# A hybrid attention/retention inference step: one more pair of channel tiles as seven products, parked sums of x through a buffer half as large

## The chip, the cores and the metric

The kernel runs on one core of a Trainium2 chip. The metric is device time in microseconds (us); the kernel before takes 1887.12 us, the median of three runs (1886.89 to 1887.62). The profiled execution took 1887.63 us, of which the profile's span, from the first instruction to the last, is 1885.9 us.

## What is computed

One encoder layer on 2048 new frames (the prompt) and 64 frames of a running stream (the sample): a norm, one wide input projection, differential attention, retention, gates, and the output projections. All data are float32. Cut to what matters here:

```python
D_MODEL, SEQ, DEC_SEQ = 1024, 2048, 64
h = rmsnorm(x, norm_g) @ w_in                       # 6144 columns in all
qa, ka, va, za, qb, kb, vb, zb, ga, gb = split(h)   # za, zb: silu gates; ga, gb: merge gates
oa = diff_attention(rmsnorm(qa), rmsnorm(ka), va)   # block-causal, 4 heads
ob = retention(qb, kb * DK_B ** -0.5, vb)           # chunkwise recurrent, 4 heads
oa = rmsnorm(oa) * (1 - lam_init) * silu(za)
ob = rmsnorm(ob) * silu(zb)
m  = sigmoid(ga + b_gate[0]) * (oa @ w_oa) + sigmoid(gb + b_gate[1]) * (ob @ w_ob)
y  = x + m @ w_out
```

The change concerns the projection columns qb, kb, za, zb, ga and gb: 16 blocks of 256 columns, called pairs here since each is two tiles of 128 channels. They are produced transposed, channels on the partitions and frames along the row.

## The kernel before

**Products.** A float32 value is held as a high and a low part (`h` and `l`, or `wh`, `wl`, `xh`, `xl`), made by a cast on ScalarE (ACT) and a subtraction on VectorE (DVE) or GpSimd (POOL). A float32 product is three matmuls: high by high, high by low, low by high.

**Stages.** The frames are worked in two halves of 1024; the second half also carries the 64 sample frames, so it has 1088 columns: 512 and twice 288. In each half the input projection runs (`w_stream`), and attention and retention (`z_stream`) fill in between its matmuls. After the second half the out stream follows (`out_stream`, L2935): gates, `m`, and `y`.

**Pairs in the first half** are all made by `strassen` (L958) with seven products of sums in place of eight blocks. The sums of weight blocks t1 to t4, formed on POOL in `sum_prep` (L805), are stored to a DRAM tensor `wsum` by `sum_keep` (L866) for those pairs that will need them again: the pairs from number `PLAIN` on.

**Pairs in the second half.** The first `PLAIN` = 11 pairs are made plainly by `transposed` (L1426, matmuls at L1137): for each of the two channel tiles, 8 blocks of the contraction and three matmuls each, over columns of 512, 288 and 288. The last five are made together by `quad` (L1544, matmuls at L1564): seven phases, in the order of `PHASES`, one product of sums each. In a phase each pair has one weight piece (`wh`, `wl`) of 4 blocks and two column groups, of 256 and of 288 columns: 12 matmuls into one bank for each. Between phases the sums stay in SBUF buffers `u256` and `u288`, 11 of each.

**What follows a product.** `q_p6` to `q_p3` (L1600 to L1650) read the bank: the first phase, S2, by a copy on ACT (L1591), the second, A11, by a copy and a DVE add (L1584), the others by one DVE add, the fifth, S3, by two. The adds go to `u` or to an evacuation tile `ev` that a DMA then stores.

**Sums of x.** `x_again` (L1479) forms the eight operands of x on POOL while attention runs and parks them in a DRAM tensor `xd`. `x_pass` (L1510) brings them back, phase by phase. The first phase's operand (S2) arrives already split. For each other phase one load (`xraw<-xd`, 1088 KB) lands in `xraw`, [128, 2176]; once one of the two slots of `xh`/`xl` is free (`xfree`, given when a phase's last matmul has been issued), four pieces of 544 are split: cast on ACT (L1526), subtraction on DVE (L1529). `quad` waits at the head of each phase for the finished slot.

**Other work around that place.** When attention has ended, `out_prep` and `load_wout` begin to prepare the out stream beside the products: `on<-on,z` (L2609 on POOL, L2615 on DVE), `ogl` (L2626), and the output weights' low parts (L2473 on POOL, L2477 on DVE). The low parts of the weight pieces (`next_sub`, L747) go to whichever of DVE and POOL the planner's own clock shows less loaded.

**What sets the order.** The instruction order of PE, ACT and DVE is written out by hand-made generators under a small planner: `loop` (L197) picks the task of lowest priority number that is ready by its clock, which advances by assumed costs (`P`, `A`, `V`, `G`, `ld`, `st`, L258 to L288). On the chip each engine takes its instructions strictly in that order. All loads and stores go out on one queue, SP's, in order.

Of the kernel before, what the change touches and what calls it, by code (L numbers as in the profile page):

```python
# [8 lines left out]
F32 = mybir.dt.float32  # L9
# [59 lines left out]
OPERANDS = [("b11", 0, 0), ("t2", 2, 1), ("t3", 0, 1), ("b21", 1, 0), ("t1", 2, 0), ("t4", 0, 0), ("b22", 1, 1)]  # L69


PLAIN = 11
SPREAD = 6000.0
PHASES = [("t2", "S2", "q_p6"), ("b11", "A11", "q_p1"), ("b21", "A12", "q_p2"), ("t1", "S1", "q_p5"),
          ("t3", "S3", "q_p7"), ("t4", "A22", "q_p4"), ("b22", "S4", "q_p3")]
NAMES = ("S2h", "A22", "A11", "A12", "S1", "S3", "S4", "S2l")
# [96 lines left out]
class Hybrid:  # L173
# [631 lines left out]
    def sum_prep(self):  # L805
# [17 lines left out]
        pair = len(self.sunits) - 1 + self.sdone  # L823
        keep = pair >= PLAIN
        left = [11 if keep else 7, 0.0]
# [600 lines left out]
    def transposed(self, dst, d0, scale, grouped):  # L1426
# [6 lines left out]
        self.nplain += 1  # L1433
        if self.nplain == PLAIN:
            order = [(ct, k) for k in (1, 2, 0) for ct in range(2)]
        for ct, k in order:
# [7 lines left out]
                                     (ct, k) == order[-1])  # L1444
            if self.nplain == PLAIN and (ct, k) == (1, 2):
                self.seg1_done = self.pe + LAT
# [63 lines left out]
    def x_pass(self):  # L1510
        self.xslots, self.xfree, self.parked, self.xraw = [], [(1, 0.0)], -1, None
        yield lambda: self.parked == 1 and self.seg1_done is not None
        yield max(self.seg1_done, self.kept)
        for k, (_, name, _) in enumerate(PHASES):
            if k == 0:
                for j, x in enumerate(self.x_slot(0)):
                    t = self.ld(x.bitcast(F32), self.xd[:, 7 * j].rearrange("p c t -> p (c t)"), 1114112)
                self.xslots.append((0, t))
                yield lambda: self.xraw is not None
                continue  # L1520
            t = self.ld(self.xraw, self.xd[:, NAMES.index(name)].rearrange("p c t -> p (c t)"), 1114112)
            s = yield from self.ring(self.xfree)
            yield t
            h, l = self.x_slot(s)
            for c in range(0, 2176, 544):
                self.nc.scalar.copy(h[:, c:c + 544], self.xraw[:, c:c + 544])  # L1526
                t = self.A(544, self.pe)
                yield t
                self.nc.vector.tensor_sub(l[:, c:c + 544], self.xraw[:, c:c + 544], h[:, c:c + 544].bitcast(F32))  # L1529
                t = self.V(644, t)  # L1530
            self.xslots.append((s, t))
            yield t

    def u_room(self):

        self.zx.close()
        pool = self.z2.enter_context(self.tc.tile_pool(name="sums", bufs=1))
        self.xraw = pool.tile([128, 2176], F32, tag="xraw", name="xraw")
        self.ufree = []
        for n in WIDTH:  # L1540
            u = pool.tile([128, 11 * n], F32, tag=f"u{n}", name=f"u{n}")
            self.ufree.append([(u[:, n * k:n * k + n], 0.0) for k in range(11)])

    def quad(self, pairs):  # L1544

# [1415 lines left out]
    def w_stream(self):  # L2961
# [31 lines left out]
        later = [(vb, lambda half: self.natural(half, self.fin_vb(), False, True), True)]  # L2993
        plain = [(c0, lambda half, a=a: self.transposed(*a), False) for c0, a in again[:PLAIN]]
        c0s, args = zip(*again[PLAIN:])
        seqs = [first + early + seq, [plain[0], wide[0], plain[1], wide[1], wide[2], m0, m1, plain[2], plain[3],
# [4 lines left out]
        for half in range(2):  # L3001
            for c0, wide in self.order[half]:
                if half:
                    self.pieces += [(wide,)] * {True: 8, False: 4, "quad": 7 * (16 - PLAIN)}[wide]
                else:
# [197 lines left out]
```

## Time and profile before

| | |
|---|---|
| runs | 1886.89, 1887.12, 1887.62 us |
| profiled execution, its own time | 1887.63 us |
| span of its profile | 1885.9 us |
| between the two | 1.73 us |
| granted TensorE clock over the span | 1.0 of full speed |
| DVE, ACT, POOL busy | 1330.5, 975.9, 669.5 us |
| matmuls of the plain pairs (L1137, `mm<-xh,wh`) at 288 columns | 352, mean 303 ns each |
| matmuls of the product block (L1564) | 840, from 1419.07 to 1532.1 us |

How to read it: a matmul's listed duration contains the pipeline behind it, so that 840 matmuls of some 290 ns overlap and cannot be added. What one costs the engine is the distance between starts. The engines' busy times are sums over stages with different limits, so a change in one stage is read from that stage: here the stretch from about 1380 us, where attention ends, to 1532 us, where the out stream starts.

### The profile page before, as it was taken

Reading aid. Unit: us, or ns where it says so; the run is one execution under the profiler, and the core shown is the slowest. Engines: PE = TensorE matmul, PEld = TensorE weight load, DVE = VectorE, ACT = ScalarE, POOL = GpSimd, SP = SyncE. Lnnn points to the kernel's source line nnn. Section 1 sums busy time; section 2 is a strip of 40 time slices with the busy share of each in tenths; the row PEclk is TensorE's granted clock in tenths of the full one; section 3 lists DMA queues with packets and bytes.
Section 4 is the critical chain, followed back from the end, with each engine's and each line's share of the span. In section 5 each row is a group of like instructions: output and inputs, shape, how many; then the busy total and the mean of one; then the engine's idle time right before and its main releaser. Section 6 shows DMA issues by size and latency. Waiting matters only on the chain.

```text
span 1885.9 us, 33029 instructions
## 1 busy us (share of the span) xinstructions
PE 1867.0 (99%) x11090; PEld 1644.9 (87%) x11090; DVE 1330.5 (71%) x3117; ACT 975.9 (52%) x2266; POOL 669.5 (36%) x723
## 2 busy tenths in 40 slices
PE   9999999999999999999999999999999999999999
PEld 7788878888888789888988889899999899998887
DVE  6765857658585677787587777677866969977664
ACT  6444545554434566556465655556666436654221
POOL 2420266555552122022210344243224625512442
PEclk9999999999999999999999999999999999999999
DMA  7664555666867967556423649446437988886452
GB/s 258 209 177 122 162 165 169 177 199 198 243 185 191 254 196 191 154 170 174 139 73 95 178 131 244 120 130 158 115 115 231 284 233 257 271 237 209 165 157 77
DMA packets 402555, 340.07 MB, mean 180 GB/s; under 512 B 85329, under 2 KB 348625, under 8 KB 401362
## 3 DMA queue, kind: packets, MB, share of 16 engines
q1 hardware_dynamic: 402386, 337.97, 61.7%
q8 instruction: 87, 1.43, 0.3%
q14 instruction: 82, 0.67, 0.1%
HBM read 218.27 MB, written 118.75 MB: 179 GB/s over the span
## 4 chain that ended last, share of the span: by engine, by line
PE 89%; DMA 4%; DVE 4%; issue 1%; SPq 1%; ACT 1%; POOL 0%; DVEq 0%; ACTq 0%; POOLq 0%
PE mm L1137 29%; PE mm L989 8%; PE tp L989 4%; PE at L1990 3%; PE s L1879 2%; PE s L1878 2%; PE s L989 2%; PE pv L1970 2%; PE pv L1969 2%; PE pv L1968 2%; PE mm L1564 1%; PE s L2793 1%; PE s L2795 1%; PE s L2794 1%; PE pv L2256 1%
## 5 line engine op out<-in xcount | busy, mean ns | idle before, releaser
L748 POOL TENSOR_TENSOR wl<-ws,wh 128x512 fp32r<-128x512 f32 x102 | 142.5, 1408 | 240.8 <-ACT wh L727 160.2
L1137 PE MATMUL mm<-wh,xh 128*128 128x512 f32 x504 | 203.0, 403 | 0.0
L1137 PE MATMUL mm<-wh,xl 128*128 128x512 f32 x504 | 198.1, 393 | 0.0
L1137 PE MATMUL mm<-wl,xh 128*128 128x512 f32 x504 | 198.0, 393 | 0.1
L1137 PE MATMUL mm<-xh,wh 128*128 128x288 f32 (+2 forms) x544 | 179.8, 330 | 0.0
L1137 PE MATMUL mm<-xh,wl 128*128 128x288 f32 (+2 forms) x544 | 175.5, 323 | 0.0
L1137 PE MATMUL mm<-xl,wh 128*128 128x288 f32 (+2 forms) x544 | 175.5, 323 | 0.0
L1918 ACT ACTIVATE row<-row,a_mx 128x1024 f32<-128x1024 f32 (+7 forms) x144 | 149.8, 1042 | 11.7 <-DVE a_mx L1897 11.7
L2006 DVE TENSOR_TENSOR atl<-at,ath 128x512 fp32r<-128x512 f32 (+1 forms) x144 | 92.6, 658 | 77.8 <-ACT ath L2004 77.6
L2004 ACT CAST ath<-at 128x512 fp32r<-128x512 f32 (+1 forms) x144 | 79.1, 564 | 106.2 <-PE at L1990 105.7
L856 POOL TENSOR_TENSOR wl<-ws,wh 128x256 fp32r<-128x256 f32 x64 | 55.3, 865 | 197.8 <-ACT wh L847 197.6
L1745 POOL TENSOR_TENSOR r_y<-r_y,r_sq 128x256 f32<-128x256 f32 x32 | 29.7, 929 | 236.2 <-DVE r_sq L1742 152.4
L1137 PEld LDWEIGHTS mm<-wh,xl 128*128 128x128 f32 x504 | 94.6, 188 | 21.6
L1137 PEld LDWEIGHTS mm<-wl,xh 128*128 128x128 f32 x504 | 95.0, 188 | 18.4 <-POOL wl L748 0.9
L1137 PEld LDWEIGHTS mm<-wh,xh 128*128 128x128 f32 x504 | 94.9, 188 | 17.8 <-DVE raw L1308 0.2
L1137 PEld LDWEIGHTS mm<-xh,wh 128*128 128x128 f32 x544 | 102.4, 188 | 7.2
L1137 PEld LDWEIGHTS mm<-xl,wh 128*128 128x128 f32 x544 | 102.5, 188 | 6.9
L1137 PEld LDWEIGHTS mm<-xh,wl 128*128 128x128 f32 x544 | 102.3, 188 | 6.6
L1887 DVE CUSTOM_DVE_ANT_0 row<-s,dfar 128x512 f32<-128x512 f32 (+2 forms) x141 | 87.0, 629 | 23.4 <-PE s L1879 16.8
L1940 DVE SCALAR_TENSOR_TENSOR row<-row,a_w 128x1024 f32<-128x1024 f32 (+5 forms) x88 | 97.3, 1111 | 0.0
L727 ACT CAST wh<-ws 128x512 fp32r<-128x512 f32 x111 | 67.7, 619 | 47.9 <-DMA ws<-wsum 13.2
L1878 PE MATMUL s<-K,q 128*128 128x512 f32 (+3 forms) x240 | 90.5, 379 | 1.3 <-DVE a_acc L1887 1.3
(543 smaller groups left out, 6072.4 us busy)
## 6 DMA issues: line engine op xcount, KB each, us to landing
ws<-in_w_in_dram SPq DMA_DIRECT2D x155, 256.0 KB, 3.4
q<-qT SPq DMA_DIRECT2D x128, 128.0 KB, 3.8
K<-kT SPq DMA_DIRECT2D x48, 256.0 KB, 4.6
V<-vN SPq DMA_DIRECT2D x24, 512.0 KB, 5.9
row<-in_x_prompt_dram SPq DMA_DIRECT2D x16, 512.0 KB, 4.5
wz<-in_w_in_dram SPq DMA_DIRECT2D x32, 256.0 KB, 4.3
row<-in_cache_k_T_dram SPq DMA_DIRECT2D x32, 256.0 KB, 3.2
row<-in_cache_v_diff_dram SPq DMA_DIRECT2D x32, 256.0 KB, 3.6
```

The lines of the kernel that those rows point to most:

```text
L727: self.nc.scalar.copy(h, st)
L748: eng.tensor_sub(l, st, h.bitcast(F32))
L856: nc.gpsimd.tensor_sub(l[:, cs], src, h[:, cs].bitcast(F32))
L989: nc.tensor.matmul(ps, w[:, c], xs[x][c], start=bool(tag) and c == 0 and i == 0, stop=c == 3 and i == 2, skip_group_check=True)
L1137: nc.tensor.matmul(ps, p, q, start=c == 0 and i == 0, stop=c == KC - 1 and i == 2)
L1878: nc.tensor.matmul(ps, q1s, kk, start=True, stop=False)
L1887: nc.vector.tensor_tensor_reduce(out=row[:, k0:k0 + n], in0=ps, in1=tab, scale=-SLOPES[h], scalar=3.0e38, op0=ALU.add, op1=ALU.min, accum_ ...
L1918: nc.scalar.activation(u, u, AF.Exp, bias=mx, scale=-1.0, accum_out=lp[:, k:k + 1])
L1940: nc.vector.scalar_tensor_tensor(out=u0, in0=u1, scalar=w[:, 0:1], in1=u0, op0=ALU.mult, op1=ALU.add)
L1990: nc.tensor.transpose(at[:, w:w + 128], src, self.ident)
L2004: nc.scalar.copy(ah[:, :w], at[:, :w])
L2006: nc.vector.tensor_sub(al[:, :w], at[:, :w], ah[:, :w].bitcast(F32))
```

## The change

`PLAIN` goes from 11 to 10: pair number 10, two tiles of `ga`, leaves the plain pairs and joins the product block, which then has six pairs. Its sums t1 to t4 are kept in `wsum` in the first half (four more stores of 256 KB), and in the second half its weights come as seven pieces of [128, 4, 128] rather than four of [128, 2, 256]. Each phase has six pairs, 144 matmuls, where it had 120. The `u` buffers go from 11 to 13 of each width; to make room `xraw` goes from 2176 to 1088 columns, and `x_pass` brings each operand in two loads, the second of which overwrites the first one's buffer, so it is issued after the first one's two pieces have been split.

```diff
-PLAIN = 11
+PLAIN = 10
@@ x_pass
-            t = self.ld(self.xraw, self.xd[:, NAMES.index(name)].rearrange("p c t -> p (c t)"), 1114112)
-            s = yield from self.ring(self.xfree)
-            yield t
-            h, l = self.x_slot(s)
-            for c in range(0, 2176, 544):
-                self.nc.scalar.copy(h[:, c:c + 544], self.xraw[:, c:c + 544])
-                t = self.A(544, self.pe)
+            for a in (0, 1088):
+                t = self.ld(self.xraw, self.xd[:, NAMES.index(name)].rearrange("p c t -> p (c t)")[:, a:a + 1088], 557056)
+                if a == 0:
+                    s = yield from self.ring(self.xfree)
+                    h, l = self.x_slot(s)
                 yield t
-                self.nc.vector.tensor_sub(l[:, c:c + 544], self.xraw[:, c:c + 544], h[:, c:c + 544].bitcast(F32))
-                t = self.V(644, t)
+                for c in (0, 544):
+                    x = self.xraw[:, c:c + 544]
+                    self.nc.scalar.copy(h[:, a + c:a + c + 544], x)
+                    t = self.A(544, self.pe)
+                    yield t
+                    self.nc.vector.tensor_sub(l[:, a + c:a + c + 544], x, h[:, a + c:a + c + 544].bitcast(F32))
+                    t = self.V(644, t)
+                yield t
             self.xslots.append((s, t))
-            yield t
@@ u_room
-        self.xraw = pool.tile([128, 2176], F32, tag="xraw", name="xraw")
+        self.xraw = pool.tile([128, 1088], F32, tag="xraw", name="xraw")
...
-            u = pool.tile([128, 11 * n], F32, tag=f"u{n}", name=f"u{n}")
-            self.ufree.append([(u[:, n * k:n * k + n], 0.0) for k in range(11)])
+            u = pool.tile([128, 13 * n], F32, tag=f"u{n}", name=f"u{n}")
+            self.ufree.append([(u[:, n * k:n * k + n], 0.0) for k in range(13)])
```

The lines after the change lie three further down in the file (L1564 becomes L1567, L1584 becomes L1587), and the split's L1526 and L1529 become L1529 and L1532.

On TensorE the order is the same up to the second of the last two plain pairs before the block, and the same again from the first matmul of the out stream on. Between, attention (queries by keys, `s<-K,q`) is found inside the product block, where before only its last transposes and value products reached into the block. Before, at the block's first matmul (`L1990` are the attention's transposes, `L1968` to `L1970` its products with V):

```order
L1968 MATMUL pv<-ath,V 128x256
L1969 MATMUL pv<-ath,V 128x256
L1970 MATMUL pv<-atl,V 128x256
L1990 MATMUL at<-ident,row 128x128 x3
L1564 MATMUL tp<-xh_122,wh 128x256
L1564 MATMUL tp<-xl_123,wh 128x256
L1564 MATMUL tp<-xh_122,wl 128x256
L1564 MATMUL tp<-xh_122,wh 128x256
```

After the change, in the block's first phase:

```order
L1567 MATMUL mm<-xl_123,wh 128x256
L1567 MATMUL mm<-xh_122,wl 128x256
L1881 MATMUL s<-K,q 128x512
L1882 MATMUL s<-K,q 128x512
L1881 MATMUL tp<-K,q 128x512
L1882 MATMUL tp<-K,q 128x512
L1567 MATMUL mm<-xh_122,wh 128x256
L1567 MATMUL mm<-xl_123,wh 128x256
```

72 matmuls of the block stand before the attention's last rows in the old order and 768 behind them; now it is 264 and 744.

On DVE the splits of x lie differently among the adds. Before, the four splits for phase A22, while phase S3 runs:

```order
L1529 TENSOR_TENSOR xl_123<-xraw,xh_122 128x544
L1584 TENSOR_TENSOR u_16726<-at,u_16726 128x256
L1529 TENSOR_TENSOR xl_123<-xraw,xh_122 128x544
L1584 TENSOR_TENSOR ev<-at,u_16726 128x256
L1584 TENSOR_TENSOR u_16727<-at,u_16727 128x288
L1529 TENSOR_TENSOR xl_123<-xraw,xh_122 128x544
L1584 TENSOR_TENSOR ev<-at,u_16727 128x288
L1584 TENSOR_TENSOR u_16726<-mm,u_16726 128x256
L748 TENSOR_TENSOR wl<-ws,wh 128x512
L1529 TENSOR_TENSOR xl_123<-xraw,xh_122 128x544
```

After the change, the last two of the four splits for that phase and what stands ahead of them:

```order
L1587 TENSOR_TENSOR ev<-mm,u_16215 128x288
L1587 TENSOR_TENSOR ev<-mm,u_16214 128x256
L1587 TENSOR_TENSOR u_16215<-s,u_16215 128x288
L748 TENSOR_TENSOR wl<-ws,wh 128x512
L1587 TENSOR_TENSOR ev<-s,u_16215 128x288
L1587 TENSOR_TENSOR u_16214<-s,u_16214 128x256
L1532 TENSOR_TENSOR xl_123<-xraw,xh_122 128x544
L2618 TENSOR_TENSOR on<-on,z 128x528
L1587 TENSOR_TENSOR u_16215<-at,u_16215 128x288
L1587 TENSOR_TENSOR ev<-s,u_16214 128x256
L1532 TENSOR_TENSOR xl_123<-xraw,xh_122 128x544
```

The splits come in two twos, and the last two stand behind more of the phase's adds. From the row after the last split for phase S1 to the last split for phase A22, the work beside phases S1 and S3, DVE has 46 rows before the change (24 adds from banks and 22 operations between SBUF tiles) and 65 after it (37 and 28); from there to the last split for S4 it has 24 rows before and 22 after (12 and 10). In the last phase-long piece ahead of A22 alone, after the change, there are 24 adds and 14 of the others.

On SP's queue, the loads of x for S3 (`gbT<-ev` are stores of finished tiles, `ws` weight pieces, `z`, `on` and `wst` for the out stream). Before, one row among the others:

```order
L280 DMA ws<-wsum 128x4x128
L280 DMA xraw<-xd 128x2176
L285 DMA gbT<-ev 128x4x8
L285 DMA gbT<-ev 128x256
L280 DMA ws<-wsum 128x4x128
L285 DMA gbT<-ev 128x256
```

After, the first load, the second one, and what lies between them:

```order
L280 DMA xraw<-xd 128x1088
L285 DMA gbT<-ev 128x256
L280 DMA ws<-wsum 128x4x128
L285 DMA gbT<-ev 128x4x8
L285 DMA gbT<-ev 128x256
L280 DMA z<-zbT 128x2x264
L280 DMA on<-obT 128x2x264
L280 DMA ws<-wsum 128x4x128
L280 DMA wst<-in_w_o_diff_dram 128x2x256
L280 DMA ws<-wsum 128x4x128 x2
L280 DMA xraw<-xd 128x1088
```

Ten transfers for other users stand between the two.

## The prediction

> **What bounds the kernel now.** I read the page first, then the chain of waits, then PE's waits and the stretches of the product block.
>
> ```profile
> span 1885.9 us, 33029 instructions
> PE 1867.0 (99%) x11090; PEld 1644.9 (87%) x11090; DVE 1330.5 (71%) x3117; ACT 975.9 (52%) x2266; POOL 669.5 (36%) x723
> PE 89%; DMA 4%; DVE 4%; issue 1%; SPq 1%; ACT 1%; POOL 0%; DVEq 0%; ACTq 0%; POOLq 0%
> ```
>
> The reader sees an engine that is hardly ever idle: 1885.9 - 1867.0 = 18.9 us over the whole span, and a chain that is PE for 89%. So fewer matmul columns shorten the run, unless PE then has to wait. Of that idle time the product block holds this (its waits, then its stretches: PE, PEld, DVE, ACT and POOL busy, clock, DMA share, GB/s):
>
> ```profile
> PE mm L1564 <- DVE ev L1584: 2.1, 1, 2.1
> PE s L1564 <- DVE xl L1529: 1.6, 1, 1.6
> PE s L1564 <- DVE u L1584: 0.9, 1, 0.9
> ...
> 1460.00:1480.00 20.00, 20.00 (x161) 19.97 (x160) 15.67 (x24) 10.35 (x18) 8.68 (x7) 1.00 0.84 238
> 1480.00:1500.00 20.00, 17.49 (x132) 16.57 (x130) 20.00 (x28) 11.07 (x19) 17.86 (x11) 1.00 1.10 330
> 1500.00:1520.00 20.00, 18.00 (x143) 18.03 (x144) 16.78 (x31) 8.15 (x15) 9.23 (x7) 1.00 1.05 274
> ```
>
> Three waits, 2.1 + 1.6 + 0.9 = 4.6 us, all on DVE, which in 1480 to 1500 us is busy without a gap. The third 2 us, in 1500 to 1520, are the wait on `ev`; elsewhere in the block PE is full. So the block has two limits close together: PE, and in phases S1 and S3 the DVE.
>
> **The change part by part. Matmuls.** What one costs is the distance between starts, twelve apart in a row:
>
> ```profile
> 1403.72 0.39 PE L1137 MATMUL mm<-xh,wl 128*128 128x512 f32 x1
> ...
> 1406.44 0.39 PE L1137 MATMUL mm<-xh,wl 128*128 128x512 f32 x1
> ...
> 1442.07 0.28 PE L1564 MATMUL mm<-xh,wh 128*128 128x256 f32 x1
> ...
> 1443.49 0.30 PE L1564 MATMUL mm<-xh,wh 128*128 128x288 f32 x1
> ...
> 1445.09 0.28 PE L1564 MATMUL s<-xh,wh 128*128 128x256 f32 x1
> ```
>
> That is 2.72/12 = 0.227 us at 512 columns, 1.42/12 = 0.118 at 256, 1.60/12 = 0.133 at 288. Removed: 2 tiles x 8 blocks x 3 = 48 at 512 and 96 at 288, 10.9 + 12.8 = 23.7 us. Added: 7 x 12 = 84 at 256 and 84 at 288, 9.9 + 11.2 = 21.1 us. Net **-2.6 us**: the seven-for-eight ratio gives 3 us, and shorter matmuls give 0.4 back. A phase becomes 6 x (1.42 + 1.60) = 18.1 us long; it was 15.1.
>
> **First half.** Four more stores of 256 KB, and one pair's raw weights held until they land. PE has no wait on a weight there today; the sums of the pairs after this one are kept in the same way. Nothing; if that cover failed, one load's time of some 4 us once.
>
> **Attention inside the block.** 192 more of the block's matmuls stand ahead of attention's end and take the place of the plain ones there in PE time (192 x 0.126 = 24 us against 23.7). Beside them ACT and DVE get copies and adds that the plain pairs hadn't. Between 1400 and 1440 us DVE was idle for half:
>
> ```profile
> 1400.00:1420.00 20.00, 20.00 (x129) 17.98 (x128) 9.38 (x19) 9.89 (x20) 6.77 (x5) 1.00 0.33 88
> 1420.00:1440.00 20.00, 20.00 (x163) 19.98 (x162) 8.94 (x13) 12.39 (x30) 7.82 (x7) 1.00 0.85 277
> ```
>
> 40.0 - 18.3 = 21.7 us of room against some 10 adds and 8 splits, 14 us. Nothing again; without that cover it is a rival below.
>
> **DVE in phases S1 and S3** is the term that decides. Its work between 1467.8 and 1502 us, by groups (count, busy us, mean ns):
>
> ```profile
> L1529 DVE TENSOR_TENSOR xl<-xraw,xh 128x544 fp32r<-128x544 f32 x8 | 10.2, 1278 | 1.9 <-ACT xh L1526 1.9
> L2477 DVE TENSOR_TENSOR w_o_retl<-wst,w_o_reth 128x512 fp32r<-128x512 f32 x4 | 4.2, 1044 | 0.6 <-ACT w_o_reth L2470 0.6
> L2477 DVE TENSOR_TENSOR w_o_diffl<-wst,w_o_diffh 128x512 fp32r<-128x512 f32 x2 | 2.9, 1446 | 0.0
> L2626 DVE TENSOR_TENSOR ogl<-on,ogh 128x528 fp32r<-128x528 f32 x2 | 2.9, 1429 | 1.8 <-ACT ogh L2623 1.8
> L1584 DVE TENSOR_TENSOR u<-mm,u 128x256 f32<-128x256 f32 (+1 forms) x6 | 2.6, 428 | 0.0
> L748 DVE TENSOR_TENSOR wl<-ws,wh 128x512 fp32r<-128x512 f32 x2 | 2.2, 1094 | 0.0
> L2615 DVE TENSOR_TENSOR on<-on,z 128x528 f32<-128x528 f32 x1 | 0.7, 699 | 0.0
> ...
> L1529 DVE TENSOR_TENSOR xl<-xraw,xh x24: 707/1102/1854, 1425.3 to 1514.7; 128x544 fp32r<-128x544 f32 x24
> ...
> L1529 DVE TENSOR_TENSOR xl<-xraw,xh 128x544 fp32r<-128x544 f32 x24 | 27.8, 1163 | 4.5 <-ACT xh L1526 4.4
> ...
> 1467.80:1502.00 34.20, 29.69 (x228) 28.77 (x227) 29.87 (x43) 18.51 (x32) 23.77 (x15) 1.00 1.05 308
> ...
> 1476.71 1.30 POOL L748 TENSOR_TENSOR wl<-ws,wh 128x512 fp32r<-128x512 f32 x1 [3.11 <-ACT wh L727]
> ```
>
> (behind them the splits' range, their mean over the whole block, the stretch as a whole, and one instruction of POOL)
>
> An add that reads a bank takes 0.43 us there, always. An operation between SBUF tiles takes 0.70 us at best (the splits' fastest is 0.707, their slowest 1.854) and here 23.1/19 = 1.22 in the mean, while POOL is busy beside it. Test on the order before: 24 adds and 22 others beside these two phases make 24 x 0.43 + 22 x 1.22 = 37.2 us. PE needs 2 x 15.1 = 30.2, and S1's last split was done some 1.9 us ahead of S1's first matmul (the rows: 1464.33 against 1466.18):
>
> ```profile
> 1462.52 1.81 DVE L1529 TENSOR_TENSOR xl<-xraw,xh 128x544 fp32r<-128x544 f32 x1
> ...
> 1466.18 0.28 PE L1564 MATMUL at<-xh,wh 128*128 128x256 f32 x1
> ```
>
> 37.2 - 30.2 - 1.9 = 5.1 us, near the 4.6 of the three waits. The order after has 37 adds and 28 others beside the same two phases: 15.9 us plus 28 x 1.22 = 34.2, together 50.1 against 36.2. Lower end: all at 0.70, 35.5 us, no excess over both, but S3 alone has 24 and 14, 20.1 against 18.1, so 2.0. Upper end 50.1 - 36.2 = 13.9, if the head start is gone. The splits' mean over the whole block is 1.16 where it is 1.28 here; scaled so, 1.22 becomes 1.11, the sum 15.9 + 31.1 = 47.0, and with half the old head start 47.0 - 36.2 - 0.9 = 9.9 us. I take **10 us of new waits**, nearer the upper end, because the work for the out stream (the `w_o` and `og` rows) falls into the same two phases as before. What is late next is the split that stands last for A22 and the adds that free banks.
>
> The Trainium skill, page "SBUF — State Buffer", section "SBUF: two separate sides", says why: VectorE, in an instruction with two SBUF inputs, and GpSimd share one port pair, and whichever starts first holds it for its whole instruction. The trace agrees: 0.71 to 1.85 us between SBUF tiles, 0.43 from a bank. By that rule what has to fit is the pair's own time: 15 POOL instructions in 34.2 us are 16 in 36.2, so 28 x 0.70 + 16 x 1.30 = 40.4 us, 4.2 over PE's 36.2, and the time would be 1884, the upper end of rival A.
>
> **The halved load.** Today's chain for one phase:
>
> ```profile
> 1485.35 0.34 SPq L280 DMA_DIRECT2D xraw<-xd  x1
> 1491.88 1.20 ACT L1526 CAST xh<-xraw 128x544 fp32r<-128x544 f32 x2 [2.02 <-DMA xraw<-xd]
> 1499.33 1.83 DVE L1529 TENSOR_TENSOR xl<-xraw,xh 128x544 fp32r<-128x544 f32 x1
> 1501.19 0.32 SPq L280 DMA_DIRECT2D xraw<-xd  x1
> ...
> xraw<-xd SPq DMA_DIRECT2D x5, 1088.0 KB, 5.9
> ws<-in_w_in_dram SPq DMA_DIRECT2D x12, 256.0 KB, 4.4
> ```
>
> 6.5 us to the first cast, then 9.3 us for four pieces, then the next load: 15.8 us. With two loads it is two landings and the same pieces. A load of 544 KB lies between 4.4 (256 KB) and 5.9 us (1088 KB); 2 x 4.4 + 9.3 = 18.1 us to 2 x 5.9 + 9.3 = 21.1 us, against a phase of 18.1. Between those ends I take 5.0 us, since most of a landing doesn't go with size in these rows: 19.3 us, 1.2 over. Beside S1 and S3 that overlaps the DVE's own lateness and isn't added; ahead of S4, where DVE has 12 x 0.43 + 10 x 1.1 = 16.2 us, it would cost about 1 us, within the rounding of the 10.
>
> The page "DMA: Bandwidth & Descriptors" of the Trainium skill, section "Anatomy of one DMA — SWDGE (gpsimd) path", puts a DMA at a fixed 2 us and bytes over 436 GB/s. By that rule half the size saves 1.3 us of 5.9: 4.6 us, 18.5 for the chain, and the sum stays.
>
> **Sum:** -2.6 (matmuls) - 4.6 (old waits, which fall into the same phases and are counted anew) + 10 (new waits) = +2.8 us. On the profiled 1887.63 that is 1890.4; that execution lay 0.5 us above the median, so 1889.9, said as **1890.0**. Measurements of this kernel tell 0.2% (3.8 us) from no change, so this is slightly slower and just within.
>
> **The rivals.**
> A. *The DVE is relieved.* A phase grows by 3 us and its four splits don't; the six adds' share of DVE is the same, so the queue could run nearer 0.70 a row and the waits stay at 0 to 4.6 us. 1887.1 - 2.6 = 1884.5 with the old waits, 1880 with none. For it: 1460 to 1480 us, where DVE has 15.67 of 20. Against: S3's 20.1 us in 18.1 even at best.
> B. *The single small buffer sets the pace* (the slower side). At 5.9 us a landing the chain is 3.0 us longer than a phase, at the heads of S1, S3, A22 and S4. In the first two it hides in the 10; in the other two it adds 6: +8.8, 1896. It decides from about 4.4 us a landing on. For it: DMA share 1.10 in that stretch, and ten other transfers between the two on SP's queue. Against: 4.4 us rows beside it.
> C. *Attention in the block stalls PE.* Attention's softmax rows on DVE hold up the adds that free three banks; two or three waits of 1 to 2 us as in the block today, +4 on the sum: 1894. For it: queries by keys now stand between products. Against: the 21.7 us of room.
> D. *The change doesn't do what it says* (it would leave the matmuls as they were): the order shows 24 matmuls more and the plain pair gone. No chance given.
>
> **How the numbers follow.** My forecast, waits of 8 to 13.9 us: 1888 to 1893.8, 0.50, of which 0.27 lies below 1890.9 and 0.23 above. A 0.25: 0.17 faster than 1883.3, 0.08 within. B 0.17, slower. C 0.08: 0.05 slower, 0.03 within. Together faster 0.17, same 0.38, slower 0.45. The range runs from half of A, 1882.0, to B with a little of the unknown above, 1898.0; the forecast's own is 1888 to 1893.8.
>
> **What would show it.** L1567 has 1008 matmuls; starts in a phase as far apart as now; block and plain pairs together 2.6 us less between waits. DVE at or near 20.00 of 20 for both of S1 and S3; PE's waits on `xl` L1532 and on `ev`, `u` L1587, 8 to 13.9 us in all. `xraw<-xd` 12 times with a median of 4.6 to 5.4 us. Waits below 5 us make me wrong by A; waits at the head of A22 and S4 above 2 us each, with ACT idle for `xraw<-xd`, by B; waits before attention's end by C; anything before the last plain pairs or behind the block, by something I don't see.

## The result, and the profile after

The changed kernel takes 1891.71 us, the median of 13 runs (1888.38 to 1893.45); the kernel before, run beside it, 1887.12 (1884.04 to 1887.90, 13 runs). The ratio is 1.0023, with a 95% interval of 1.0016 to 1.0030: 4.6 us slower by the medians, just over what can be told from no change. The profiled execution took 1893.45 us, the slowest of the 13.

The page of the changed kernel, its span and its engines:

```profile
span 1891.5 us, 33139 instructions
PE 1870.7 (99%) x11114; PEld 1649.1 (87%) x11114; DVE 1330.4 (70%) x3130; ACT 976.0 (52%) x2267; POOL 675.7 (36%) x727
```

PE has 24 matmuls more and, of 5.6 us more span, 3.7 us more "busy". The totals don't say where they went. The groups of PE's matmuls with first and last start (count, shortest, median and longest ns, then the two times) do: the last of the retention's transposes ahead of the block, and the first of the out stream behind it.

```profile
L2411 PE MATMUL pv<-ident,row x32: 222/272/273, 917.0 to 1269.4; 128*128 128x128 f32 x28, 64*128 64x64 f32 x4
L2672 PE MATMUL s<-ogh,w_o_diffh x64: 279/283/289, 1537.9 to 1718.2; 128*128 128x264 f32 x64
```

From the one to the other there are 1537.9 - 1269.4 = 268.5 us; in the kernel before, the same two places (its L2408 and L2669) stand at 1269.8 and 1532.2, 262.4 us apart. So +6.1 us lies between them, all of the difference and a little more. PE's waits from 1372 to 1540 us (total us, times, longest):

```profile
PE at L1567 <- DVE xl L1532: 5.0, 6, 1.7
PE at L1567 <- ACT xh L1529: 3.2, 1, 3.2
PE mm L1567 <- ACT u L1594: 0.3, 1, 0.3
```

None of the three old waits is left (two of them on `ev` and `u`); 8.5 us of others stand there, nearly all on the splits of x. In PE's timeline they stand at the heads of three phases, S3, A22 and S4 (start, duration, what ran, and in brackets the wait ahead of it):

```profile
1472.59 0.38 PE L1567 MATMUL at<-xl,wh 128*128 128x256 f32 x1 [1.29 <-DVE xl L1532]
1474.18 0.39 PE L1567 MATMUL at<-xl,wh 128*128 128x256 f32 x1 [0.97 <-DVE xl L1532]
...
1494.42 0.39 PE L1567 MATMUL at<-xl,wh 128*128 128x256 f32 x1 [0.37 <-DVE xl L1532]
1496.78 0.38 PE L1567 MATMUL at<-xl,wh 128*128 128x256 f32 x1 [1.66 <-DVE xl L1532]
...
1517.88 0.38 PE L1567 MATMUL at<-xh,wh 128*128 128x256 f32 x1 [3.24 <-ACT xh L1529]
1518.64 0.38 PE L1567 MATMUL at<-xl,wh 128*128 128x256 f32 x1 [0.38 <-DVE xl L1532]
1519.61 0.58 PE L1567 MATMUL at<-xl,wh 128*128 128x256 f32 x1 [0.35 <-DVE xl L1532]
```

That is 2.26 us at S3, 2.03 at A22 and 3.97 at S4. Here is the chain that made the last two late, in the timelines of SP, ACT and DVE: for A22 the first five rows, for S4 the five behind the dots.

```profile
1474.15 0.34 SPq L280 DMA_DIRECT2D xraw<-xd  x1
1480.37 0.65 ACT L1529 CAST xh<-xraw 128x544 fp32r<-128x544 f32 x1 [2.57 <-DMA xraw<-xd]
1488.89 0.38 SPq L280 DMA_DIRECT2D xraw<-xd  x1
1492.96 0.65 ACT L1529 CAST xh<-xraw 128x544 fp32r<-128x544 f32 x1 [1.89 <-DMA xraw<-xd]
1495.60 1.12 DVE L1532 TENSOR_TENSOR xl<-xraw,xh 128x544 fp32r<-128x544 f32 x1
...
1500.76 0.46 SPq L280 DMA_DIRECT2D xraw<-xd  x1
1506.27 1.19 ACT L1529 CAST xh<-xraw 128x544 fp32r<-128x544 f32 x2 [3.86 <-DMA xraw<-xd]
1510.42 0.49 SPq L280 DMA_DIRECT2D xraw<-xd  x1
1517.18 1.19 ACT L1529 CAST xh<-xraw 128x544 fp32r<-128x544 f32 x2 [2.84 <-DMA xraw<-xd]
1518.84 0.72 DVE L1532 TENSOR_TENSOR xl<-xraw,xh 128x544 fp32r<-128x544 f32 x1
```

For A22, from the issue of the first load to the end of the last split, 1474.15 to 1496.72, there are 22.6 us, and a phase of PE is 18.1. For S4 it is 1500.76 to 1519.56, 18.8 us, but its first load is issued 4.0 us after the buffer came free at 1496.72. And the stretches of the last three phase heads, first the two of S1 and S3, then the one ahead of S4 (length, then PE, PEld, DVE, ACT and POOL busy, clock, DMA share, GB/s):

```profile
1456.00:1474.00 18.00, 15.92 (x126) 15.51 (x124) 14.22 (x21) 10.60 (x19) 10.20 (x7) 1.00 1.02 301
1474.00:1492.00 18.00, 17.82 (x129) 17.83 (x130) 18.00 (x31) 9.30 (x17) 15.04 (x9) 0.91 0.91 266
...
1500.00:1510.00 10.00, 10.00 (x82) 10.00 (x81) 5.55 (x10) 3.70 (x7) 3.93 (x3) 1.00 1.11 304
1510.00:1520.00 10.00, 6.04 (x43) 5.44 (x43) 5.27 (x11) 3.60 (x6) 3.69 (x3) 0.96 0.88 214
```

DVE is full in S3 alone. In the first stretch it is busy for 14.22 of 18, and in S1 proper (1452.4 to 1470.5, before S3's matmuls begin) for 13.74 of 18.1. Ahead of the longest wait, at S4, it is busy for half the time: there neither DVE nor ACT is short, only the data are missing.

The clock column holds something that the profiled execution of the kernel before, with 1.0 all along, didn't have. In stretches of 3.40 us around the waits of S3 and S4:

```profile
1471.40:1474.80 3.40, 1.24 (x8) 1.04 (x9) 3.40 (x8) 3.23 (x7) 0.36 (x1) 1.00 0.90 270
1474.80:1478.20 3.40, 3.40 (x17) 3.40 (x16) 3.40 (x3) 2.31 (x5) 3.40 (x3) 0.51 0.97 286
1515.80:1519.20 3.40, 0.95 (x4) 0.60 (x4) 1.34 (x3) 1.76 (x3) 0.37 (x1) 1.00 0.86 198
1519.20:1522.60 3.40, 3.05 (x13) 3.00 (x13) 1.14 (x3) 0.05 (x1) 1.42 (x2) 0.50 1.01 278
```

After a stretch with 1.24 or 0.95 us of PE work, the next one runs at half the clock: 17 matmuls in 3.40 us where 82 in 10.00 us (the row from 1500 on) would make 28. Half of 3.4 us is 1.7 us lost each time, some 3.4 us for the two by this estimate, without a row in the list of waits. A third such stretch of this profile, from 618.1 us on, lies in the first half, ahead of the places compared above.

The kernel before isn't free of them either. Over the whole span, the changed kernel's 13 runs have a granted clock of 0.996 to 0.999, 0.997 in the median; 83 runs of the kernel before, timed beside the experiments below, have 0.997 to 1.0, 0.999 in the median. The changed kernel has more of it, but how much more the two profiles alone don't say.

### The profile page after: what moved, and what is told of

Its sections match the earlier page's. It is cut to its first block, busy times and chain, and to the rows that moved or that the text cites. A ratio compares the mean times of both kernels' runs of the same rounds, so it can differ in the third digit from the quotient of the medians.

```text
span 1891.5 us, 33139 instructions
## 1 busy us (share of the span) xinstructions
PE 1870.7 (99%) x11114; PEld 1649.1 (87%) x11114; DVE 1330.4 (70%) x3130; ACT 976.0 (52%) x2267; POOL 675.7 (36%) x727
## 4 chain that ended last, share of the span: by engine, by line
PE 62%; DMA 2%; DVE 1%; SPq 1%; ACT 1%; issue 1%; POOL 0%; DVEq 0%; POOLq 0%; ACTq 0%
PE mm L1137 20%; PE at L1993 3%; PE s L1881 2%; PE s L1882 2%; PE mm L1567 2%; PE pv L1973 2%; PE pv L1972 2%; PE pv L1971 2%; PE s L2796 1%; PE s L2798 1%; PE s L2797 1%; PE s L1567 1%; PE s L2673 1%; PE mm L2672 1%; PE at L2672 1%; SPq L280 1%
## 5 line engine op out<-in xcount | busy, mean ns | idle before, releaser
L748 POOL TENSOR_TENSOR wl<-ws,wh 128x512 fp32r<-128x512 f32 x106 | 148.8, 1414 | 259.4 <-ACT wh L727 188.2
L1137 PE MATMUL mm<-xh,wh 128*128 128x288 f32 (+2 forms) x496 | 163.9, 330 | 0.0
L1137 PE MATMUL mm<-xh,wl 128*128 128x288 f32 (+2 forms) x496 | 159.9, 322 | 0.0
L1137 PE MATMUL mm<-xl,wh 128*128 128x288 f32 (+2 forms) x496 | 159.8, 322 | 0.0
L1890 DVE CUSTOM_DVE_ANT_0 row<-s,dfar 128x512 f32<-128x512 f32 (+2 forms) x141 | 87.3, 629 | 25.1 <-PE s L1882 19.5
L1137 PEld LDWEIGHTS mm<-xh,wh 128*128 128x128 f32 x496 | 93.4, 188 | 6.3
L1137 PEld LDWEIGHTS mm<-xl,wh 128*128 128x128 f32 x496 | 93.5, 189 | 6.1
L1137 PEld LDWEIGHTS mm<-xh,wl 128*128 128x128 f32 x496 | 93.3, 188 | 6.1
```

The source lines that it names most:

```text
L748: eng.tensor_sub(l, st, h.bitcast(F32))
L1137: nc.tensor.matmul(ps, p, q, start=c == 0 and i == 0, stop=c == KC - 1 and i == 2)
L1890: nc.vector.tensor_tensor_reduce(out=row[:, k0:k0 + n], in0=ps, in1=tab, scale=-SLOPES[h], scalar=3.0e38, op0=ALU.add, op1=ALU.min, accum_ ...
```

## The experiments

Two theories stood against each other. L: the chain of load, two splits, load, two splits through the small buffer is longer than a phase and sets its head. D: the work of DVE in S1 and S3, the prediction's deciding term, makes the splits late. All twelve kernels were timed against the kernel before on their own chip, so ratios are compared:

| kernel | median us | ratio to before, 95% |
|---|---|---|
| the changed kernel | 1891.71 | 1.0023 (1.0016 to 1.0030) |
| before, four more stores | 1888.31 | 1.0003 (0.9993 to 1.0012) |
| five pairs, small buffer | 1904.72 | 1.0094 (1.0081 to 1.0107) |
| changed, 12 adds fewer | 1889.87 | 1.0018 (1.0009 to 1.0027) |
| six pairs, x in place | 1886.57 | 1.0001 (0.9993 to 1.0010) |
| five pairs, x in place | 1893.12 | 1.0027 (1.0015 to 1.0038) |
| x in place, 12 adds fewer | 1886.61 | 0.9998 (0.9989 to 1.0007) |
| changed, fill of ones | 1895.34 | 1.0039 (1.0026 to 1.0052) |
| changed, fill of weights | 1894.53 | 1.0041 (1.0029 to 1.0053) |
| changed, w_o spread | 1886.70 | 1.0004 (0.9996 to 1.0013) |
| before, w_o spread | 1885.37 | 0.9994 (0.9984 to 1.0003) |
| x in place, w_o spread | 1883.71 | 0.9977 (0.9968 to 0.9986) |
| x in place in two loads, w_o spread | 1879.36 | 0.9961 (0.9949 to 0.9974) |

**The stores of the first half.** The kernel before, keeping one more pair's sums:

```diff
-        keep = pair >= PLAIN
+        keep = pair >= PLAIN - 1
```

> The kernel before with only the four more stores of sums in the first half (they are read by nobody). Both theories: no effect, 1886.5 to 1887.7 us; half clock in the first half in its profile, as the changed kernel's has at 611 us, would say that the stores bring it, then 1888.8 us.

1.0003: nothing that can be told, as the prediction had it.

**The small buffer without the sixth pair.** The changed kernel with

```diff
-PLAIN = 10
+PLAIN = 11
```

and 11 `u` buffers of each width:

> Only the second part of the change: five pairs as before, but x through the half buffer in two loads. Theory L (the chain of load, split, load, split through one small buffer sets the pace; 22.6 us from load to load for A22 in the changed kernel): a phase is 15.1 us here, so PE waits 4 to 7 us at each of the four last heads, 16 to 28 us, 1903 to 1915 us. Theory D (DVE has too much to do beside S1 and S3, the half buffer is harmless): the DVE's work is that of before, 1887 to 1889 us.

1.0094, some 18 us slower than before and 13 slower than with the sixth pair. PE's waits in the block:

```profile
PE mm L1567 <- ACT xh L1529: 4.8, 1, 4.8
PE mm L1567 <- DVE xl L1532: 4.4, 5, 1.4
PE s L1567 <- DVE xl L1532: 3.6, 3, 1.7
PE s L1567 <- ACT xh L1529: 1.9, 1, 1.9
```

Together with two small ones 16.2 us, all on the splits of x. This kernel has fewer adds on DVE and still waits twice as long: its phases are 15.1 us, 3.0 us shorter, and the chain has the same links: for S1, S3 and A22 it takes 18.3, 15.6 and 19.5 us, each longer than a phase. That is as L has it. The reader sees also what the sixth pair is worth beside the small buffer: not its 2.6 us of matmuls alone, but 3 us more cover for the chain in each phase.

**DVE relieved.** The changed kernel without the add `u3`, 12 instructions in S3 (12 x 0.43 = 5.2 us of DVE):

```diff
-        q["u3"] = t = self.q_scaled(q["b"], ps, q["b"], scale, q["n"], t)
+        q["u3"] = t = max(t, q["t5"])
```

> The changed kernel without one of the two adds of phase S3 for each group (the sum u3 is left out, so the lower tiles of the block are not the reference's): 12 adds of 0.43 us, 5.2 us, less on DVE in that phase, loads as they are. Theory D: the wait at the head of A22 (some 2 us, with a clock drop behind) goes, 1887 to 1889 us. Theory L: the chain of loads is as long, at most 1 us less, 1890.5 to 1892 us.

```profile
PE at L1567 <- DVE xl L1532: 5.3, 6, 1.8
PE at L1567 <- ACT xh L1529: 2.1, 1, 2.1
```

7.4 us where there were 8.2, and the ratio falls by 0.0005, within the intervals. By D most of it should have gone. But the run relieves DVE less than it was meant to. From the last split for S1 to the last for A22 DVE is busy for 39.7 of 45.1 us; in the changed kernel it is 40.7 of 45.6. The adds take 3.7 us less there, and the rows between SBUF tiles 2.7 us more. And A22's chain is as long as it was, 22.6 us: from the first cast to the second load it takes 6.8 us in place of 8.5, but the second load then takes 6.7 us to its cast in place of 4.1. So this run alone doesn't decide against D; the next one and the burst of `w_o` do.

**No buffer.** The six pairs again; x lands in one load of 1088 KB in the low half of the free slot and is split where it lies:

```diff
-            for a in (0, 1088):
-                t = self.ld(self.xraw, ...[:, a:a + 1088], 557056)
...
+            s = yield from self.ring(self.xfree)
+            h, l = self.x_slot(s)
+            t = self.ld(l.bitcast(F32), ..., 1114112)
+            yield t
+            for c in range(0, 2176, 544):
+                x = l[:, c:c + 544].bitcast(F32)
```

> Six pairs, but no landing buffer: one load of 1088 KB brings the operand into the low half of its own slot once that is free, and the split is made in place. DVE and ACT do the same work. Theory L: from free slot to last split about 6 us of load and 7 to 9 us of splits, 13 to 15 us, in a phase of 18.1: the waits at the heads of A22 and S4 (8.5 us in all with S3's) go, and the half-speed clock after them: 1880 to 1883 us. Theory D: the waits on xl stay, 1889 to 1892 us.

1.0001, between the two forecasts: 4 us better than the changed kernel, not under the kernel before. PE's waits on `ev` and `x`, and DVE's wait of 5.58 us, which stands behind the second wait on `ev`:

```profile
PE at L1565 <- DVE ev L1585: 3.6, 2, 1.9
PE at L1565 <- DVE xl L1530: 0.7, 1, 0.7
...
1504.18 0.46 DVE L1585 TENSOR_TENSOR ev<-at,u 128x288 f32<-128x288 f32 x1 [5.58 <-DMA gbT<-ev]
```

With every add of DVE still there, and DVE busy for 40.5 of the 42.7 us between the same two splits, the waits on x fall from 8.2 to 0.7 us: the work of DVE is the same, the second landing is gone. What comes up in their place is an add that waited 5.58 us for a store to give back its `ev` tile. Another 1.3 us are waits on rows of other work (`r_sq`, `atl`), and the clock is 0.91 from 1500 to 1520.

The same landing with five pairs:

> Five pairs as before, without the buffer xraw: x lands in one load of 1088 KB in the low half of the free slot and is split in place. If the number of matmuls is what the sixth pair is worth, this stands 2.6 us above the in-place kernel with six pairs, 1889 us less the wait on xl of 1.6 us that goes: 1886 to 1888 us. If the sixth pair's additions and evacuations cost what its matmuls save, both are the same: 1884 to 1886.5 us.

```profile
PE mm L1565 <- DVE xl L1530: 3.8, 3, 2.9
PE at L1565 <- DVE xl L1530: 2.7, 1, 2.7
...
xl<-xd SPq DMA_DIRECT2D x5, 1088.0 KB, 6.2
```

1.0027, slower than either forecast said: a phase of 15.1 us is again too short, here for a load of 6.2 us that can begin only when the slot is free, and four splits. Against six pairs it is 0.0026, 4.9 us, and the matmuls are 2.6 of that.

And the in-place kernel with six pairs, without `u3`:

> The in-place kernel with six pairs, without the addition u3 of the pairs (one of their sums is left out, so part of the output is not the reference's). If DVE's work is the second limit once the small buffer is gone (the waits on ev of 3.6 us), the waits shrink: 1882.5 to 1884.5 us, 2 to 4 us under 1886.6. If the waits on ev come from stores behind a full DMA queue, DVE's relief changes nothing: 1886 to 1887 us.

0.9998, no gain that can be told. The waits on `ev` shrink from 3.6 to 0.2 us, but 4.3 us on `xl` come up in their place. DVE's adds alone aren't the second limit either.

**The burst of w_o.** Three quarters of the output weights are loaded and split beside the last phases. One line puts 14 us of the planner's clock ahead of each:

```diff
             if g == 0:
                 for q in range(1, 4):
+                    yield self.pe + 14000
                     yield from self.load_wo(q)
```

In the changed kernel:

> The changed kernel with 14 us put by the planner between the quarters of w_o, and nothing else. If the two loads through the small buffer set the pace whatever else is on the DMA queue: within 1 us of the changed kernel, 1890.5 to 1893 us. If the loads of xd were late because of the burst of w_o loads beside them: 1886 to 1889 us, as the same spread took 3 to 4 us from the in-place kernel.

1.0004: one line takes 0.0019, some 3.6 us, from the changed kernel, nearly all of its loss. Its waits on x are 5.3 us, 1.65 at S3 and 3.63 at A22, and none is at S4. The place is the first load for S4. On SP's queue of the changed kernel, from the end of A22's last split (1496.72 us):

```profile
1496.80 0.38 SPq L280 DMA_DIRECT2D ws<-in_w_in_dram  x1
1497.28 1.74 SPq L285 DMA_DIRECT2D gbT<-ev  x3
...
1500.22 0.44 SPq L280 DMA_DIRECT2D ws<-in_w_in_dram  x1
1500.76 0.46 SPq L280 DMA_DIRECT2D xraw<-xd  x1
```

and with the spread, DVE's last split for A22 and the load:

```profile
1492.14 1.79 DVE L1532 TENSOR_TENSOR xl<-xraw,xh 128x544 fp32r<-128x544 f32 x1
1493.96 0.33 SPq L280 DMA_DIRECT2D xraw<-xd  x1
```

Seven other transfers stood ahead of the load (the three rows and, behind the dots, one of `z` and one of `on`), 4.0 us; with the spread it is issued 0.03 us after the split. The changed kernel's wait at S4 is 3.97 us. The loads hadn't been slowed by the burst beside them (from 1420 to 1535 us their median is 4.4 us in both); the burst moved the place of the load in the order. None of the seven is a load of `w_o` itself: what the line changes is the order that the planner writes.

The spread also relieves DVE, whose rows for `w_o` lie elsewhere. Ahead of A22, first the changed kernel, then with the spread:

```profile
1480.00:1490.00 10.00, 10.00 (x82) 10.00 (x81) 10.00 (x20) 5.57 (x10) 7.87 (x5) 1.00 0.88 249
1480.00:1490.00 10.00, 9.27 (x74) 9.07 (x72) 6.61 (x16) 2.11 (x4) 3.88 (x3) 1.00 1.03 277
```

From the last split for S1 to the last for A22 DVE is busy for 36.0 of 44.8 us, 4.7 us less than in the changed kernel. Yet A22's chain is as long, 22.7 us, and the wait at its head is 3.63 us where it was 2.03. The step from the first cast to the second load shrinks from 8.5 to 5.5 us, and the second load takes 6.4 us to its cast in place of 4.1; why it takes longer here and without `u3`, the runs don't show. This is the test of D: DVE is relieved, and the wait at A22 stays.

In the kernel before:

> The kernel before (five pairs, buffer of full size) with 14 us put by the planner between the quarters of w_o, and nothing else. If the spread helps whichever way x lands (3.6 us from the changed kernel, about 4 from the in-place one): 1882 to 1884.5 us, and the changed kernel's loss against it stays. If it helps only where the landing of x is short of time, as the kernel before has only 1.6 us of waits on xl: 1886 to 1888 us, and the sixth pair's worth is to be read from the spread in-place kernels.

0.9994, less than can be told. So the spread isn't a gain of its own: it pays where the landing of x is short of time.

**The half clock.** The changed kernel with 31 matmuls of ones into an unused bank at the heads of S3, A22 and S4:

```diff
                     for c in range(4):
+                        if i == 0 and g == 0:
+                            for _ in range({("S3", 2): 5, ("S3", 3): 4, ("A22", 2): 1, ("A22", 3): 7,
+                                            ("S4", 0): 13, ("S4", 3): 1}.get((name, c), 0)):
+                                fill = self.psum("pv")
+                                nc.tensor.matmul(fill[:, 0:128], self.ones, self.ones, start=True, stop=True)
```

> The changed kernel with 31 small matmuls of ones (128x128, into a bank that is read by nobody before it is written again) put ahead of the first products of chunks of S3, A22 and S4, where TensorE waits for the x splits: 9 in S3, 8 in A22, 14 in S4. The x chain is untouched, so the products start no earlier. If the half-speed stretches of the clock (3.4 us each, two in the block of the changed kernel's profile) follow from TensorE's idleness, they go from the block: 1888 to 1890 us, 2 to 3.4 us under the changed kernel. If they are not bound to idleness, or cost nothing, or the fill's own time is as long as what it saves: 1891 to 1893 us.

1.0039: each took two records of 0.275 us, 17 us in all, so it was mis-sized. In its profile S3 and S4 have no half-speed stretch any more, but one of 6.8 us from 1494 on stands at A22, after 4 us with 3.08 of PE work. The second fill, `wh[:, 0]` with all of `wh`:

> The changed kernel with the same 31 extra matmuls ahead of the same products, now of a weight tile with itself (128x128 by 128x512, fp32r, 0.227 us each by the row of the 512-wide ones), 7.0 us in all, which lie in the 7.9 us of waits at those places; the 31 of ones took 2 x 0.275 us each, 17 us, and were too long for them. If the half-speed stretches in the block follow from TensorE's idleness, they go: 1888 to 1890 us. If they stay, or if the fill delays the products by its own length: 1891 to 1895 us.

1.0041, and mis-sized as well: each lasted 0.50 us and the next one's weights waited for it; all write one bank, which may be why but isn't shown. But the clock can be read. Stretches of this kernel over the three heads:

```profile
1470.00:1478.00 8.00, 6.84 (x32) 4.26 (x31) 8.00 (x13) 6.09 (x11) 4.52 (x3) 1.00 0.95 290
1494.00:1502.00 8.00, 6.71 (x34) 4.46 (x33) 6.75 (x11) 2.47 (x4) 5.34 (x4) 1.00 1.09 290
1514.00:1526.00 12.00, 11.31 (x55) 7.40 (x54) 4.49 (x9) 3.70 (x7) 4.40 (x3) 1.00 0.72 189
```

With PE kept busy the granted clock is 1.00 throughout these stretches, and 1.0 over the whole span in all five runs; the changed kernel's 13 runs have 0.996 to 0.999. So in the block the half-speed stretches go with PE's idleness; how much of it is needed the two fills don't settle. The stretch at 618 us is gone from this profile too, though nothing was filled there, so the clock over the whole span isn't the fill's doing alone. What the half-speed stretches cost by the medians stays open too, since the fill cost more than it saved.

**A version that beats both.** The in-place kernel with the spread:

> The in-place kernel with six pairs, with 14 us put by the planner between the quarters of w_o that are prepared for the out stream at the end of the block, so that their loads and splits do not meet the last x load and the ev stores. If the waits on ev come from that burst, they go: 1881 to 1884.5 us, under both kernels. If the out stream then starts late for want of w_o: 1890 us and more. If neither: 1886 to 1887 us.

0.9977, under both. Then x in two loads into the two halves of the slot, both issued at once:

```diff
-            t = self.ld(l.bitcast(F32), ..., 1114112)
-            yield t
+            ts = [self.ld(l.bitcast(F32)[:, a:a + 1088], ...[:, a:a + 1088], 557056)
+                  for a in (0, 1088)]
             for c in range(0, 2176, 544):
+                yield ts[c // 1088]
```

> The in-place kernel with six pairs and spread w_o, with x in two loads of 544 KB into the two halves of the slot, both issued when the slot is free. Splits can begin when the first half has landed (4.4 us) rather than after 6 to 9 us. If the chain of load and splits still sets the heads of the phases (waits on xl of 3.2 us left), these shrink: 1880 to 1883 us. If not: 1883 to 1885 us.

1879.36 us, 0.9961: 7.4 us under the kernel before and 12 under the changed one, a little better than its best forecast. PE's only wait on x, and the chain for A22 on SP, ACT and DVE:

```profile
PE mm L1566 <- DVE xl L1531: 0.5, 1, 0.5
...
1473.42 0.90 SPq L280 DMA_DIRECT2D xl<-xd  x2
1479.88 1.20 ACT L1528 CAST xh<-xl 128x544 fp32r<-128x544 f32 x2 [2.92 <-DMA xl<-xd]
1485.85 1.12 DVE L1531 TENSOR_TENSOR xl<-xl,xh 128x544 fp32r<-128x544 f32 x1
```

1473.42 to 1486.97 is 13.6 us, well inside a phase of 18.1, where the changed kernel took 22.6 and the in-place kernel with the spread, in one load, 15.7. The second landing no longer follows the first two splits. What is next is one wait of 1.5 us in the out stream, on the gate `ga`.

## Why the prediction came out as it did

The total came out near the forecast, 1890.0 against 1891.71, and the waits, 8.5 us, within the likeliest case's 8 to 13.9. But only 4.3 us of them came up to the head of A22, where the 10 were forecast; 4.0 came at S4, where next to nothing was, and the cause wasn't the one given.

| step | predicted us | measured us |
|---|---|---|
| matmuls | -2.6 | -2.6 by count and pace |
| old waits | -4.6 | -4.6, all three gone |
| new waits from DVE's work beside S1 and S3, up to the head of A22 | 10 | 2.3 at S3, 2.0 at A22 |
| wait at S4 for the halved load | about 1, within the rounding | 4.0 |
| half-speed clock | not seen | 3.4 in the profiled run |
| first half, attention in the block | 0 and 0 | 0 and 0.3 |

The measured terms make -2.6 - 4.6 + 8.5 + 3.4 = +4.7 of the +6.1 us of the stretch; 1.4 us isn't accounted for.

**Matmuls: right.** L1567's count is the 1008 that was said, in tiles of the same two widths, and where PE doesn't wait, 82 start in 10.00 us, 0.122 each, near the 0.118 and 0.133.

**"DVE in phases S1 and S3 is the term that decides": this step failed.** Only S3 had DVE full; S1 had 13.74 of 18.1 and no wait at its head. The sum was also too large: the 65 rows took 40.7 us, not 47.0 to 50.1, since the 28 between SBUF tiles took 0.93 us in the mean (26.1 us) and not 1.22. Over PE's 36.2 us that leaves 4.5, which looks like the 4.3 us at S3 and A22, but the runs don't bear it out as the cause: the in-place kernel has the same work of DVE, 40.5 us, and 0.7 us of waits on x in all; with the spread DVE has 36.0 us, and the wait at A22 grew. The sum of DVE's instructions was read as if PE had to wait for it. DVE counts where a split stands behind its other rows: in A22's chain that is some 5 us (1.8 ahead of the first split, 2.3 ahead of the second, 0.9 ahead of the last).

**"The halved load", left within the rounding: the term that was mis-sized.** Its landing was priced too high, at 5.0 us; the loads took less:

```profile
xraw<-xd SPq DMA_DIRECT2D x12, 544.0 KB, 4.2
```

By the rule of the page "DMA: Bandwidth & Descriptors" of the Trainium skill, section "Anatomy of one DMA — SWDGE (gpsimd) path", half the size saves 1.3 us; the estimate of 4.6 that this gave from the measured 5.9 was nearer. The section is about transfers issued from GpSimd, and these go out on SP's queue. But a landing isn't all that lies between issue and cast, and the 9.3 us of splits don't stay 9.3 when they come in two bouts: A22's chain has 6.2 us to the first cast, 8.5 from there to the second load, 4.1 to its cast, and 3.8 to the end, 22.6 in place of 19.3. And the term had no place for the queue: SP issued S4's first load 4.0 us after the buffer was free. The prediction quoted as evidence for rival B that ten other transfers stand on SP's queue between the two loads, and then gave them no price.

So **rival B's path is what happened**, with the signs that were named for it: waits at the heads of A22 and S4 of 2.03 and 3.97 us, 6.0 together, as B had it, with ACT idle ahead of them for `xraw<-xd`. B's price was wrong, though. It counted on 5.9 us a landing and said that it decides from about 4.4 on; the landings took 4.2, and the chain was long by the splits' wait for their turn on DVE and, at S4, by the load's wait for its turn on SP. B's total was too high, 1896, since it kept the 10 of DVE beside its own 6. That the forecast's total fits is thus partly chance: 10 us of a wrong cause stood for 8.3 of the right one, and 3.4 of half clock beyond.

Rival A fell: it allowed 4.6 us of waits, and there are 8.5, though its premise held in part, as DVE's rows between SBUF tiles ran nearer 0.70 than the forecast had them. Rival C fell too; ahead of attention's end there is one wait of 0.3 us. The 1884 us by the rule of the Trainium skill, page "SBUF — State Buffer", section "SBUF: two separate sides", didn't come either; no run here tells how much of DVE's time that rule accounts for.

## What to carry to other kernels

- A smaller landing buffer that is filled twice turns one landing per phase into a serial chain of two, and the second load pays its place in the queue again. Price the whole chain from the issue to the last split against the phase it hides behind, each issue with what stands ahead of it, before adding up an engine's work.
- An engine that is full in a stretch isn't yet what the next stretch waits for: take its work away, or the suspected buffer, and see which of the two moves the wait. Look in the profile whether the work is really gone: 12 adds fewer left DVE nearly as busy as it was.
- Where a buffer must go, look whether data can land at its final place: here that, two loads issued together, and other loads moved out of the way turned +4 us into -7.

## What the runs showed of the hardware

Two waits of 1.29 and 0.97 us were enough for the granted clock to fall to half for the next 3.4 us: none of the idle times was as long as such a stretch. So by this estimate a wait of some 2 us can cost nearly twice its length. Not every one does: the 2.03 us of waits at A22 brought no drop, and in stretches of 3.41 us laid from the first drop on they fall into two, with 2.79 and 1.91 us of PE work. The three half-speed stretches of the changed kernel's profile begin at 618.1, 1474.8 and 1519.2 us, 251 and 13 times 3.413 us apart, as if on a fixed grid. The Trainium skill, page "TensorE: Matmul & The Clock Gate", section "What's actually happening", has a free-running window of 3413 ns and half the clock after an idle one. The length agrees with the 3.4 us here; but the window ahead of the drop held 1.24 us of work in one case and 0.95 in the other, so a window that is partly idle does it too. How little work is too little isn't settled: with the fill of ones the clock fell after 4 us with 3.08 of PE work.
